# A streaming-encoder trunk in fp32: every other modulation unit of the first FFN's stage is loaded into the hf buffer

## Chip, cores and metric

One Trainium2 chip, one of its cores. The time is the device time of one execution in microseconds (us), the median of several runs.

## The reference

x is 256 frames of 1024 channels, c one vector of 1024. Two layers; in each a half-step SwiGLU FFN, a token mixer (layer 0 a pooling mixer, layer 1 a gated short convolution) and a second half-step FFN. Each of these three sub-layers is preceded by an RMS norm whose output is modulated from c:

```
cond = silu(c)
for i in range(2):
    mod = (cond @ ada_w[i] + ada_b[i]).reshape(B, 3, 3, 1024)
    shift, scale, gate = mod[:, :, 0], mod[:, :, 1], mod[:, :, 2]
    h = rms_norm(x, g[i, 0]) * (1 + scale[:, 0]) + shift[:, 0]
    a, b = split(h @ ffn_w_in[i, 0]);  x = x + 0.5 * gate[:, 0] * ((silu(a) * b) @ ffn_w_out[i, 0])
    ...   # the mixer, then the second FFN, in the same way
return rms_norm(x, final_g)
```

ada_w is 2 x 1024 x 9216; the hidden width of an FFN is 2816. Everything is fp32.

## The kernel before, in words

x lies transposed in SBUF, channels on 128 partitions in 8 blocks of 256 frames. All weights come from HBM in units of 1 MB, 128 partitions by 2048 elements (`UNIT`), one DMA each, all issued by SyncE (SP) in the order in which the program is written. SP issues in order: a DMA that has to wait for its buffer holds up those behind it. There are two sorts of units.

A weight unit goes through three engines. It lands in a buffer of the ring `raw` (4 buffers, `raw_unit`, L195). ACT casts it to a rounded `hi` (L239), DVE forms `lo = raw - hi` (L246, in the first product in two halves, L618 and L623), and PE multiplies three times for each product (`mm3`: hi with the high part hh of the activations, lo with hh, hi with the low part hl). The raw buffer is free when lo is done.

A modulation unit (`ada_unit`, L285, and `ada_first`, L289) lands in a buffer of the same ring. DVE alone reads it: `dot` (L262) multiplies it in place with cond and sums, two dots of 1024 elements a unit. Then its buffer is free.

The first FFN's first product (`ffn_start`) runs over the 8 blocks of channels (kb). Each block needs its own modulation unit (`ada_first(kb)`), from which DVE forms t (L359) and ACT hh (L360), and its weights. Block 0 is done in plain fp32: ACT writes the modulated activations into the buffer `hf`, and PE multiplies hf with the raw weights (16 products, 32 records in the profile). `second()` of a block is the second half of its work: for block 0 it copies hf into hh and hl (L608, L609), for the others it forms the second half of lo (L623) and issues the second half of the matmuls. It is called inside the next block's pass, so on DVE L623 of block 1 stands behind the dots and t of block 2:

```
for kb in range(KB):
    if kb:
        ada_first(kb)
    ...
    low_part = modulated(0, 0, kb, rstd, hh)
    second()
    low_part()
    high(1, 2)
    ...
```

The rest of the first FFN takes one weight unit after the other (14 more of its input weights, 11 of its output weights). In `swiglu` and `out_product`, `slot` calls `ada_unit` for later sub-layers, 18 units spread over 22 places, and 6 more come at the end of the stage. Each unit's DMA is written at the point of the program where its buffer is handed out.

hf (128 x 8 x 257 elements, L158) is used at the start for squares, then for block 0. Afterwards nothing touches it until, in the output product, `pool_shift_by_token` (L738) has ACT write the pooling mixer's shift into it (L741), and the stage's last residual writes the scaled x there.

Of the kernel before, what the change touches and what calls it, by code (L numbers as in the profile page):

```python
# [20 lines left out]
UNIT = 2048  # L21
# [96 lines left out]
def trunk(ctx: ExitStack, tc: tile.TileContext, calls, consts: bass.AP, c_in: bass.AP,  # L118
          x_in: bass.AP, fg_in: bass.AP, wall: bass.AP, out: bass.AP):
    nc = tc.nc  # L120
# [8 lines left out]
    def bank(name):  # L129
        return ps.tile([P, 2, T], F32, tag="bank", name=name)  # L130
# [4 lines left out]
    def mm(dst, w, m, start, stop):  # L135
        PE.matmul(dst, w, m, start=start, stop=stop, skip_group_check=True)  # L136

    def mm3(dst, w, m, start, stop):

        mm(dst, w[0], m[0], start, False)  # L140
        mm(dst, w[1], m[0], False, False)
        mm(dst, w[0], m[1], False, stop)
# [15 lines left out]
    hf = one.tile([P, KB, T + 1], F32, name="hf")  # L158
# [33 lines left out]
    gh = one.tile([P, FC, T], F32R, name="gh")  # L192
    gl = one.tile([P, FC, T], F32R, name="gl")

    def raw_unit(*call, tag="raw"):  # L195
        u = len(calls)
        calls.append(call)
        t = wp.tile([P, UNIT], F32, tag=tag, name=f"raw{u}", bufs=NRAW if tag == "raw" else NSPLIT)
        nc.sync.dma_start(t, wall[u])
        return t  # L200
# [6 lines left out]
    def unit(i):  # L207
        while len(units) <= i:
            call, at = todo.pop(0)
            if isinstance(at, str):  # L210
                raw = raw_unit(*call, tag=at)
                units.append((call, raw, None, None))
                continue
            raw = raw_unit(*call)
            if not gap:

                gap.append(wp.tile([P, BEHIND], F32, tag="gap", name="gap", bufs=1))
                G.memset(gap[0], 0.0)
            if at is None:
                parts = [wp.tile([P, UNIT], F32R, tag=n, name=f"{n}{len(units)}") for n in ("hi", "lo")]  # L220
            else:
                parts = [g[:, at : at + KB].rearrange("p b t -> p (b t)") for g in (gh, gl)]
            units.append((call, raw, *parts))
        return units[i]

    def spans(parts):
        n = UNIT // parts
        return [slice(p * n, (p + 1) * n) for p in range(parts)]
# [6 lines left out]
    def high(n, parts=1):  # L235

        for _, raw, hi, _ in next_of("hi", n):
            for at in spans(parts) if hi else ():
                S.copy(hi[:, at], raw[:, at])  # L239

    def low(n, parts=1):

        high(n, parts)
        for _, raw, hi, lo in next_of("lo", n):
            for at in spans(parts) if hi else ():
                V.tensor_sub(lo[:, at], raw[:, at], hi[:, at].bitcast(F32))  # L246

    def take(kind, pattern, **sizes):
        call, raw, hi, lo = units[done["used"]]
        assert call[0] == kind and done["lo"] > done["used"], (call, kind, done)  # L250
        units[done["used"]] = None
        done["used"] += 1
        if hi is None:
            return raw.rearrange(pattern, **sizes)
        return hi.rearrange(pattern, **sizes), lo.rearrange(pattern, **sizes)
# [8 lines left out]
    def mod_dots(layer, sub, mod, w, lo):  # L264

        key, n = (layer, sub, mod), w.shape[1]
        if key not in mods:
            mods[key] = one.tile([P, KB], F32, name=f"mod{layer}{sub}{mod}")
        b = ada_col(layer, sub, mod) + lo
        for i in range(n):  # L270
            dot(mods[key][:, lo + i : lo + i + 1], w[:, i], cst[:, b + i : b + i + 1])
        mod_finish(key, lo, n)

    def mod_finish(key, lo, n):
# [7 lines left out]
        elif mod == GATE and layer == 0:  # L282
            V.tensor_mul(m, m, cst[:, C_PS + lo : C_PS + lo + n])

    def ada_unit(layer, sub, mod, q):  # L285
        raw = raw_unit("ada", layer, sub, mod, q).rearrange("p (b n) -> p b n", b=2)
        mod_dots(layer, sub, mod, raw, 2 * q)

    def ada_first(kb):  # L289
        raw = raw_unit("ada0", kb).rearrange("p (m n) -> p m n", m=2)  # L290
        mod_dots(0, 0, SCALE, raw[:, 0:1], kb)
        mod_dots(0, 0, SHIFT, raw[:, 1:2], kb)

# [13 lines left out]
    def ada_next(n):  # L307
        for _ in range(n):
            ada_unit(*ada_todo.pop(0))
# [44 lines left out]
    def modulated(layer, sub, k, rstd, to):  # L354


        scale, shift = (mods[layer, sub, m][:, k : k + 1] for m in (SCALE, SHIFT))
        t = wk.tile([P, T], F32, tag="t", name=f"t{layer}{sub}{k}", bufs=4)
        V.scalar_tensor_tensor(t, x[:, k], scale, rstd, ALU.mult, ALU.mult)  # L359
        S.activation(to[:, k, :T], t, AF.Identity, bias=shift)  # L360
        return lambda: V.scalar_tensor_tensor(
            hl[:, k], t, shift, hh[:, k, :T].bitcast(F32), ALU.add, ALU.subtract
        )
# [10 lines left out]
    def h_pair(k):  # L374
        return hh[:, k, :T], hl[:, k]
# [179 lines left out]
    def swiglu_pair(cs, banks, name):  # L555
        sa, g = ({c: wk.tile([P, T], F32, tag=n, name=f"{n}{name}{c}") for c in cs} for n in ("sa", "g"))
        for c in cs:
            S.activation(sa[c], banks[c][:, 0], AF.Silu)
        for c in cs:
            V.tensor_mul(g[c], sa[c], banks[c][:, 1])  # L560
        for c in cs:
            S.copy(gh[:, c], g[c])
        for c in cs:
            V.tensor_sub(gl[:, c], g[c], gh[:, c].bitcast(F32))
# [17 lines left out]
    def ffn_start(rstd, name):  # L582

        banks = [bank(f"{name}b{c}") for c in range(NFIRST)]
        half = NFIRST // 2

        def product(kb, w, cs):
            for c in cs:
                for s in range(2):
                    mm3(banks[c][:, s], (w[0][:, c, s], w[1][:, c, s]), h_pair(kb),  # L590
                        kb == 0 and s == 0, kb == KB - 1)

        second = lambda: None
# [3 lines that stand above are left out]
            call, raw, hi, lo = unit(kb)  # L597
            if hi is None:
                modulated(0, 0, kb, rstd, hf)
                second()  # L600
                low(1)
                w = take("ffn_first", "p (c s n) -> p c s n", c=NFIRST, s=2)
                for c in range(NFIRST):
                    for s in range(2):
                        mm(banks[c][:, s], w[:, c, s], hf[:, kb, :T], kb == 0 and s == 0, kb == KB - 1)

                def second(kb=kb):
                    S.copy(hh[:, kb, :T], hf[:, kb, :T])  # L608
                    V.tensor_sub(hl[:, kb], hf[:, kb, :T], hh[:, kb, :T].bitcast(F32))  # L609

                continue
            low_part = modulated(0, 0, kb, rstd, hh)
# [3 lines that stand above are left out]
            done["lo"] += 1  # L616
            at, bt = spans(2)
            V.tensor_sub(lo[:, at], raw[:, at], hi[:, at].bitcast(F32))  # L618
            w = take("ffn_first", "p (c s n) -> p c s n", c=NFIRST, s=2)
            product(kb, w, range(half))  # L620

            def second(kb=kb, w=w, raw=raw, hi=hi, lo=lo):
                V.tensor_sub(lo[:, bt], raw[:, bt], hi[:, bt].bitcast(F32))  # L623
                product(kb, w, range(half, NFIRST))

        second()
        low(1)
        high(2)
        pairs = [lambda c=c: swiglu_pair((c, c + 1), banks, name) for c in range(0, NFIRST, 2)]
        pairs.pop(0)()  # L630
        low(2)
        high(3)
        ada_next(1)
        return NFIRST, pairs
# [57 lines left out]
    def ffn(layer, f, after, ahead, ready=lambda: None, between=lambda b: None, before=lambda u: None,  # L692
            rstd=None, groups=None, feed=None):
        sub, name = 2 * f, f"f{layer}{f}"
        if rstd:
            at, pairs = ffn_start(rstd, name)
        elif feed:
            at, pairs = ffn_fed(layer, f, sub, name, feed, 3, FILL)
        else:
            at, pairs = ffn_early(layer, f, sub, name, groups)  # L700
# [27 lines left out]
    def pool_means():  # L728
        S.copy(mh[:, :, 0, :EDGE], cst[:, C_E:C_M].rearrange("p (g v) -> p g v", g=4))
# [5 lines left out]
        V.tensor_mul(acc[:, :, :n], acc[:, :, :n], at)  # L735

    def pool_shift_by_token():
        pool_means()  # L738
        shift = mods[0, 1, SHIFT]
        for k in range(KB):  # L740
            S.activation(hf[:, k, :P], ones, AF.Identity, bias=shift[:, k : k + 1], scale=0.0)  # L741
# [137 lines left out]
    for p in range(2):  # L879
        b = bank(f"c{p}").rearrange("p a t -> p (a t)")  # L880
# [6 lines left out]
    rstd = rstd_of("s")  # L887
    table(AF.Silu)
    ada_first(0)

    steady = [4] * (LAST - 2)
# [74 lines left out]
```

## Time and profile before

| | us |
|---|---|
| runs shown | 863.17, 872.11, 862.32; median 863.17 |
| profiled execution | 863.46 |
| its span, first to last instruction | 861.5 |
| PE busy | 841.8 (98%) |
| DVE busy | 714.6 (83%) |
| ACT busy | 418.3 (49%) |
| granted TensorE clock, mean | 0.998 |
| read from HBM | 233.49 MB, 272 GB/s over the span |

PE's share counts matmuls from start to a modelled end, one overlapping the next, so a stretch in which PE looks busy is best judged by the number of its instructions in it. SPq rows are the issue of a DMA by SP; when it landed is another column. A wait is idle time of an engine, put down to what came last before it went on.

### The profile page before, as it was taken

What the parts mean: (1) busy time and instruction counts of PE and PEld (TensorE: products, weight loads), DVE (VectorE), ACT (ScalarE), POOL (GpSimd) and SP (SyncE); (2) the same over time, 40 slices, a digit from 0 to 9 for tenths busy, and PEclk for the clock granted to TensorE, in tenths of its full rate; (3) what the DMA queues carried; (4) which work ended last, traced back from release to release, by engine and by line L of the source; (5) the groups of instructions that cost most, each with busy time, mean ns of one, the idle gap of its engine ahead of it and who ended that gap; (6) DMA issues with size and microseconds to landing.
All of it is one profiled execution on the core that took longest, in us unless ns stands there. A gap on an engine that the chain in (4) does not pass through costs nothing.

```text
span 861.5 us, 16344 instructions
## 1 busy us (share of the span) xinstructions
PE 841.8 (98%) x6940; PEld 822.8 (96%) x6940; DVE 714.6 (83%) x1018; ACT 418.3 (49%) x538; POOL 8.4 (1%) x25
## 2 busy tenths in 40 slices
PE   4999999999999999999999999999999999999997
PEld 2999999999899999999999999999999999999886
DVE  6989999877889987878888988879887789755784
ACT  5355455343655444446644444356444756444422
POOL 3000000000000000000000000000000000000000
PEclk9999999999999999999999999999999999999999
DMA  8898899989548998886389989983465449954601
GB/s 343 335 344 322 301 350 379 370 347 385 178 165 320 372 341 321 350 310 237 105 331 350 377 310 337 363 321 148 161 228 180 190 145 343 331 192 165 224 22 49
DMA packets 33338, 235.59 MB, mean 273 GB/s; under 512 B 3697, under 2 KB 3825, under 8 KB 4978
## 3 DMA queue, kind: packets, MB, share of 16 engines
q1 hardware_dynamic: 33266, 234.56, 73.6%
q8 instruction: 54, 0.88, 0.4%
q14 instruction: 18, 0.15, 0.0%
HBM read 233.49 MB, written 1.05 MB: 272 GB/s over the span
## 4 chain that ended last, share of the span: by engine, by line
PE 85%; DVE 7%; DMA 5%; ACT 1%; issue 1%; SPq 0%; ACTq 0%
PE accf L136 21%; PE f01b L136 13%; PE f10b L136 13%; PE f11b L136 11%; PE acco L136 7%; PE f00b L136 4%; DMA raw<-wall 4%; PE pcv L136 4%; DVE raw L262 3%; PE accc L136 3%; DVE lo L246 2%; PE pe L136 2%; PE pb L136 2%; PE f01a L136 1%; PE f11a L136 1%; PE accz L136 1%
## 5 line engine op out<-in xcount | busy, mean ns | idle before, releaser
L239 ACT CAST hi<-raw 128x2048 fp32r<-128x2048 f32 (+1 forms) x151 | 263.9, 1762 | 132.5 <-DMA raw<-wall 77.5
L246 DVE TENSOR_TENSOR lo<-raw,hi 128x2048 fp32r<-128x2048 f32 (+1 forms) x137 | 298.9, 2194 | 33.1 <-ACT hi L239 32.9
L262 DVE CUSTOM_DVE_ANT_0 raw<-raw,cond,cst 128x1024 f32<-128x1024 f32 x144 | 179.6, 1281 | 12.5 <-DMA raw<-wall 12.2
L136 PE MATMUL accf<-gh,hi 128*128 128x256 f32 x528 | 145.9, 276 | 0.0
L136 PE MATMUL accf<-gh,lo 128*128 128x256 f32 x528 | 145.9, 276 | 0.0
L136 PE MATMUL accf<-gl,hi 128*128 128x256 f32 x528 | 145.8, 276 | 0.0
L136 PEld LDWEIGHTS accf<-gh,lo 128*128 128x128 f32 x528 | 99.1, 188 | 0.2
L136 PEld LDWEIGHTS accf<-gh,hi 128*128 128x128 f32 x528 | 99.1, 188 | 0.0
L136 PEld LDWEIGHTS accf<-gl,hi 128*128 128x128 f32 x528 | 99.1, 188 | 0.0
L136 PE MATMUL f00b<-hh,lo 128*128 128x256 f32 x336 | 93.1, 277 | 1.2 <-DVE lo L246 0.8
L136 PE MATMUL f00b<-hh,hi 128*128 128x256 f32 x336 | 93.1, 277 | 0.4 <-DVE gf L560 0.4
L136 PE MATMUL f00b<-hl,hi 128*128 128x256 f32 x336 | 92.8, 276 | 0.0
L136 PE MATMUL f11b<-hh,lo 128*128 128x256 f32 (+1 forms) x320 | 88.5, 277 | 0.3 <-DVE lo L246 0.3
L136 PE MATMUL f11b<-hh,hi 128*128 128x256 f32 (+1 forms) x320 | 88.4, 276 | 0.0
L136 PE MATMUL f11b<-hl,hi 128*128 128x256 f32 x320 | 88.4, 276 | 0.0
L136 PE MATMUL f10b<-hh,lo 128*128 128x256 f32 x320 | 88.3, 276 | 0.0
L136 PE MATMUL f10b<-hh,hi 128*128 128x256 f32 x320 | 88.3, 276 | 0.0
L136 PE MATMUL f10b<-hl,hi 128*128 128x256 f32 x320 | 88.3, 276 | 0.0
L136 PE MATMUL f01b<-hl,hi 128*128 128x256 f32 x304 | 84.6, 278 | 0.0
L136 PE MATMUL f01b<-hh,hi 128*128 128x256 f32 x304 | 84.2, 277 | 0.0
L136 PE MATMUL f01b<-hh,lo 128*128 128x256 f32 x304 | 83.9, 276 | 0.0
L136 PEld LDWEIGHTS f00b<-hh,lo 128*128 128x128 f32 x336 | 63.1, 188 | 1.8 <-DVE lo L246 1.0
(234 smaller groups left out, 1856.5 us busy)
## 6 DMA issues: line engine op xcount, KB each, us to landing
raw<-wall SPq DMA_DIRECT2D x221, 1024.0 KB, 6.0
x<-xt SPq DMA_DIRECT2D x4, 256.0 KB, 4.1
out<-x SPq DMA_DIRECT2D x4, 256.0 KB, 2.1
rows<-fg SPq DMA_DIRECT2D x1, 512.0 KB, 8.3
cst<-consts SPq DMA_DIRECT2D x1, 176.0 KB, 4.8
cond<-cvec SPq DMA_DIRECT2D x1, 4.0 KB
```

Of the source, the lines that this page charges most:

```text
L136: PE.matmul(dst, w, m, start=start, stop=stop, skip_group_check=True)
L239: S.copy(hi[:, at], raw[:, at])
L246: V.tensor_sub(lo[:, at], raw[:, at], hi[:, at].bitcast(F32))
L262: V.tensor_tensor_reduce(w, w, cond, 1.0, init, ALU.mult, ALU.add, out)
```

## The change

`raw_unit` gets an argument `home`: a buffer that it loads into in place of one of the ring. While a flag is on, every other call of `ada_unit` and `ada_first` passes the first 2048 elements of hf as home, the first call with the flag on included. The flag goes on in block 0's `second()`, behind the two instructions that read hf there, and off where `pool_shift_by_token` begins.

```diff
-    def raw_unit(*call, tag="raw"):
+    def raw_unit(*call, tag="raw", home=None):
         u = len(calls)
         calls.append(call)
+        if home is not None:
+            nc.sync.dma_start(home, wall[u])
+            return home
         t = wp.tile([P, UNIT], F32, tag=tag, name=f"raw{u}", bufs=NRAW if tag == "raw" else NSPLIT)
         nc.sync.dma_start(t, wall[u])
         return t
...
+    spare = {"on": False, "turn": 0}
+
+    def home():
+        if not spare["on"]:
+            return None
+        spare["turn"] += 1
+        return hf.rearrange("p k t -> p (k t)")[:, :UNIT] if spare["turn"] % 2 else None
+
     def ada_unit(layer, sub, mod, q):
-        raw = raw_unit("ada", layer, sub, mod, q).rearrange("p (b n) -> p b n", b=2)
+        raw = raw_unit("ada", layer, sub, mod, q, home=home()).rearrange("p (b n) -> p b n", b=2)
         mod_dots(layer, sub, mod, raw, 2 * q)
 
     def ada_first(kb):
-        raw = raw_unit("ada0", kb).rearrange("p (m n) -> p m n", m=2)
+        raw = raw_unit("ada0", kb, home=home()).rearrange("p (m n) -> p m n", m=2)
...
                 def second(kb=kb):
                     S.copy(hh[:, kb, :T], hf[:, kb, :T])
                     V.tensor_sub(hl[:, kb], hf[:, kb, :T], hh[:, kb, :T].bitcast(F32))
+                    spare["on"] = True
...
     def pool_shift_by_token():
+        spare["on"] = False
         pool_means()
```

The order of the weight transfers on SP stays; what they write and wait for changes. Before, from the first weight transfer on (raw0, raw2, raw4 and raw6 are the modulation units of blocks 0, 1, 2 and 3; raw1, raw3, raw5 and raw7 the weights of these blocks; in brackets the engines and earlier DMAs that a transfer waits for):

```order
L199 DMA raw0_148<-wall 128x2048
L199 DMA raw1_163<-wall 128x2048
L199 DMA raw2_184<-wall 128x2048 [waits DMAHW0_49]
L199 DMA raw3_189<-wall 128x2048 [waits DMAHW1_49]
L199 DMA raw4_228<-wall 128x2048 [waits DMAHW2_49]
L199 DMA raw5_233<-wall 128x2048 [waits DMAHW6_49,DMAHW3_49,DVE_49]
L199 DMA raw6_293<-wall 128x2048 [waits DMAHW4_49,DMAHW0_49,DVE_49]
L199 DMA raw7_298<-wall 128x2048 [waits DMAHW5_49,DMAHW2_49,DVE_49]
L199 DMA raw8_358<-wall 128x2048 [waits DMAHW1_49,DVE_49]
```

Of the changed kernel, the same place on SP:

```order
L202 DMA raw0_148<-wall 128x2048
L202 DMA raw1_163<-wall 128x2048
L202 DMA raw2_184<-wall 128x2048 [waits DMAHW0_49]
L202 DMA raw3_189<-wall 128x2048 [waits DMAHW1_49]
L199 DMA hf_82<-wall 128x2048 [waits DMAHW2_49,DVE_49,PE_49]
L202 DMA raw5_232<-wall 128x2048 [waits DMAHW3_49]
L202 DMA raw6_292<-wall 128x2048 [waits DMAHW6_49,DMAHW4_49]
L202 DMA raw7_297<-wall 128x2048 [waits DMAHW5_49,DMAHW0_49]
L199 DMA hf_82<-wall 128x2048 [waits DMAHW2_49,DVE_49]
```

The modulation unit of block 2, fifth in the row, waits for DVE and PE, and the three transfers behind it wait for no engine any more.

DVE of the changed kernel, from the end of block 1's first half on (mod001 and mod000 are the scale and shift of this sub-layer, t002 belongs to block 2, lo1 and lo2 are the low parts of the weights of blocks 1 and 2):

```order
L632 TENSOR_TENSOR lo1_194<-raw3_189,hi1_193 128x1024
L265 ISA hf_82,mod001_150<-hf_82,cond_73,cst_80 128x1024
L265 ISA mod001_150 128x1
L282 SCALAR_TENSOR_TENSOR mod001_150<-mod001_150,cst_80 128x1
L265 ISA hf_82,mod000_153<-hf_82,cond_73,cst_80 128x1024
L265 ISA mod000_153 128x1
L372 SCALAR_TENSOR_TENSOR t002_236<-x_75,mod001_150,rstds_142 128x256
L637 TENSOR_TENSOR lo1_194<-raw3_189,hi1_193 128x1024
L374 SCALAR_TENSOR_TENSOR hl_116<-t002_236,mod000_153,hh_115 128x256
L632 TENSOR_TENSOR lo2_235<-raw5_232,hi2_234 128x1024
```

Nothing moved on DVE; the two dots of block 2 read hf in place of raw4, and the second half of lo1 (L623 before, L637 now) stands behind them as it did.

## Rows read from the trace of the kernel before

**Rows 1.** The page, busy time of the engines: us, share of the span, instructions.
```profile
span 861.5 us, 16344 instructions
PE 841.8 (98%) x6940; PEld 822.8 (96%) x6940; DVE 714.6 (83%) x1018; ACT 418.3 (49%) x538; POOL 8.4 (1%) x25
```

**Rows 2.** The waits of PE in the whole span: engine and line, what it waited for, us in total, times, the longest.
```profile
PE f00b L136 <- ACT hf L360: 5.8, 1, 5.8
...
PE f00b L136 <- DVE lo L246: 0.8, 1, 0.8
PE f00b L136 <- DVE gf L560: 0.4, 1, 0.4
PE f00b L136 <- DVE lo L623: 0.4, 1, 0.4
PE f11b L136 <- DVE lo L246: 0.3, 1, 0.3
```

**Rows 3.** PE in two stretches: from:to, us, busy us (instructions), granted clock, DMA share, GB/s.
```profile
26.00:105.00 79.00, 77.35 (x675) 1.00 0.90 331
105.00:400.00 295.00, 295.00 (x2460) 1.00 0.87 324
```

**Rows 4.** The chain of work that ended last, in order of time: start, us, what.
```profile
104.69 38.27 PE f00b L136 x335
```

**Rows 5.** Waits for transfers of weights: engine and line, what it waited for, us in total, times, the longest.
```profile
ACT hi L239 <- DMA raw<-wall: 77.5, 34, 6.5
...
DVE raw L262 <- DMA raw<-wall: 12.2, 14, 1.8
```

**Rows 6.** Timeline of SP, single issues of weight transfers: start, us, engine, line, operation.
```profile
5.80 0.46 SPq L199 DMA_DIRECT2D raw<-wall  x1
...
15.50 0.33 SPq L199 DMA_DIRECT2D raw<-wall  x1
...
18.50 0.33 SPq L199 DMA_DIRECT2D raw<-wall  x1
...
24.54 0.33 SPq L199 DMA_DIRECT2D raw<-wall  x1
...
192.20 0.33 SPq L199 DMA_DIRECT2D raw<-wall  x1
192.62 1.65 SPq L199 DMA_DIRECT2D raw<-wall  x1
```

**Rows 7.** DMA issues in the windows of the issues at 5.80, 24.54, 192.20 and 192.62 us, in this order: size, us from issue to landing.
```profile
raw<-wall SPq DMA_DIRECT2D x1, 1024.0 KB, 14.6
...
raw<-wall SPq DMA_DIRECT2D x1, 1024.0 KB, 5.0
...
raw<-wall SPq DMA_DIRECT2D x1, 1024.0 KB, 5.2
...
raw<-wall SPq DMA_DIRECT2D x1, 1024.0 KB, 8.3
```

**Rows 8.** Timeline of DVE, blocks 1 to 3 and the low part of block 7: start, us, engine, line, operation, out<-in.
```profile
19.74 0.43 DVE L609 TENSOR_TENSOR hl<-hf,hh 128x256 fp32r<-128x256 f32 x1 [0.87 <-ACT hh L608]
...
21.83 1.28 DVE L262 CUSTOM_DVE_ANT_0 raw<-raw,cond,cst 128x1024 f32<-128x1024 f32 x1
...
24.43 0.48 DVE L359 SCALAR_TENSOR_TENSOR t<-x,mod,rstds 128x256 f32<-128x256 f32 x1
24.83 1.22 DVE L623 TENSOR_TENSOR lo<-raw,hi 128x1024 fp32r<-128x1024 f32 x1
25.97 0.47 DVE L361 SCALAR_TENSOR_TENSOR hl<-t,mod,hh 128x256 fp32r<-128x256 f32 x1
26.42 1.23 DVE L618 TENSOR_TENSOR lo<-raw,hi 128x1024 fp32r<-128x1024 f32 x1
27.57 1.28 DVE L262 CUSTOM_DVE_ANT_0 raw<-raw,cond,cst 128x1024 f32<-128x1024 f32 x1
...
33.33 1.28 DVE L262 CUSTOM_DVE_ANT_0 raw<-raw,cond,cst 128x1024 f32<-128x1024 f32 x1
...
56.97 1.23 DVE L618 TENSOR_TENSOR lo<-raw,hi 128x1024 fp32r<-128x1024 f32 x1
```

**Rows 9.** The instructions on the raw buffers up to 40 us, PE's matmuls of block 0 among them: count, ns min/median/max, first and last start in us.
```profile
L136 PE MATMUL f00b<-hf,raw x32: 379/379/794, 16.5 to 25.6; 128*128 128x256 f32 x32
```

**Rows 10.** PE in the stretch of block 1's first half, matmuls of f00b alone, columns as in rows 3.
```profile
25.60:28.30 2.70, 2.70 (x24) 1.00 0.87 322
```

**Rows 11.** PE around block 0, columns as in rows 3.
```profile
10.70:16.40 5.70, 0.00 (x0) 1.00 1.01 425
16.40:21.00 4.60, 4.54 (x11) 1.00 1.01 427
21.00:25.60 4.60, 4.60 (x23) 1.00 0.78 315
```

**Rows 12.** PE at the end of the span, columns as in rows 3.
```profile
855.00:856.00 1.00, 0.23 (x2) 1.00 0.45 176
...
857.00:858.00 1.00, 0.00 (x0) 0.74 0.00 0
858.00:859.00 1.00, 0.00 (x0) 0.50 0.14 55
```

**Rows 13.** Timeline of DVE, the first dots of two modulation units that land in hf in the changed kernel.
```profile
140.26 1.28 DVE L262 CUSTOM_DVE_ANT_0 raw<-raw,cond,cst 128x1024 f32<-128x1024 f32 x1
...
148.62 1.29 DVE L262 CUSTOM_DVE_ANT_0 raw<-raw,cond,cst 128x1024 f32<-128x1024 f32 x1
```

**Rows 14.** Timeline, DVE's step behind the last dots that the changed kernel makes in hf, and ACT's writes of the shift into hf.
```profile
176.36 0.16 DVE L283 TENSOR_TENSOR mod<-mod,cst 128x2 f32<-128x2 f32 x1
...
180.01 2.46 ACT L741 ACTIVATE hf<-ones,mod 128x128 f32<-128x128 f32 x8
```

## The prediction

> **What bounds the kernel now.** I read the page's busy shares first: TensorE (PE) is busy 98% of an 861.5 us span [rows 1]. A busy PE can still be a waiting one, so next came the list of waits, filtered to PE [rows 2]. The reader should see how short it is. Apart from the start (5.8 us until the first block's activations are there), the whole kernel holds four waits of PE, 0.8, 0.4, 0.4 and 0.3 us. Then I counted PE's instructions by stretch [rows 3]: 675 in the 79 us from 26 to 105 us, and from 105 to 400 us no idle time at all. In the chain that ended last, read in order of time, nothing but PE stands from 104.69 us on for hundreds of microseconds; its first piece gives PE's pace, 38.27 us for 335 matmuls, 0.114 us each [rows 4]. At that pace 79 us hold 692 matmuls, so 17 are missing, 1.9 us; the three waits in that stretch sum to 1.6 us, the same thing seen from the other side.
>
> So a better supply of weights in the first FFN can give back 1.6 us at most. A delay of PE in this stage, on the other hand, is passed on whole to the end, because there is no PE idle time behind it to absorb it. DVE and ACT do wait for transfers (12.2 and 77.5 us in all, [rows 5]), but those waits cost time only where PE waits behind them.
>
> **What the change moves.** The number of transfers, their size and all arithmetic stay as they are: 12 of the modulation units (blocks 2, 4 and 6 of the first product, and 9 later ones) land in hf and not in a raw buffer. Their dots have the same shape and I cost them at nothing (the rows of the dot below differ by 0.1 us at most, either way). The order list shows what does change. SP issues in order, and its fifth weight transfer, the modulation unit of block 2, now waits for PE and DVE, where before it waited for neither.
>
> *What it waits for.* Before, this transfer was issued at 5.80 us [rows 6] and landed 14.6 us later [rows 7], at 20.4 us, so DVE could begin its dot at 21.83 us with no wait [rows 8]. Now hf must first be free. Its last readers are DVE's subtraction at 19.74 us [rows 8], done at 20.2, and PE's 32 block-0 records, which run from 16.5 to 25.6 us plus 0.38 us [rows 9]. The later end decides: issue at 26.0 us, 20.2 us later than before. Behind it on SP stand the weights of block 2, the modulation unit of block 3 and the weights of block 3; before, these were issued at 15.5, 18.5 and 24.54 us [rows 6].
>
> *When it lands.* A transfer issued into a queue with little in it took 5.0 us (issue 24.54) and 5.2 us (issue 192.20); one issued 0.4 us behind that took 8.3 us [rows 6, 7], so they come through in order. At 26.0 us the queue is empty, since what went out ahead of this transfer had landed by 20.4 us. I take 5.0 us: hf has landed at 31.0 us, and the weights of block 2, the second of the burst, 8.3 us after 26.4, at 34.7 us. If it takes 8.3, add 3.3 us.
>
> *Who waits behind it.* DVE is in order too. Behind the two dots of block 2 stand t (L359) and then the second half of block 1's low part (L623), which PE needs for the second half of block 1. In the rows the dots start at 21.83, t at 24.43, L623 at 24.83, and the next step at 25.97 [rows 8]: 2.60, 0.40 and 1.14 us. From 31.0 us this gives 33.6, 34.0 and 35.1 us.
>
> *What PE does.* It starts block 1 at 25.6 us, and the 24 matmuls of its first half last until 28.3 us [rows 10]. Before, it went straight on. Now it stands until 35.1 us: a stall of 6.8 us. **Term 1: +6.8 us.**
>
> *The clock.* Twice the trace shows PE idle. From 10.7 to 16.4 us it did nothing; in the next 4.6 us it got through 11 records, in the 4.6 us after that through 23 of the same kind [rows 11]. The clock column says 1.00 in both, but the pace halves; I believe the pace. After the last matmul (in 855 to 856 us) the column itself shows 0.74 in 857 to 858 and 0.50, which is 1.2 GHz, from 858 us [rows 12]. An idle stretch of 6.8 us is longer than the one before 16.4 us, so I expect the same price after it: 12 records fewer in 4.6 us, or 2.4 us. **Term 2: +2.4 us**, bounds 0 (no fall) and 2.4. The Trainium skill (TensorE: Matmul & The Clock Gate, "Why this matters for your kernels") warns of drops to half clock after idle gaps between bursts of matmuls, the rule that speaks against this change; by it the sum holds term 2, without it the term is 0. The end of this trace agrees.
>
> *What comes back.* Block 2's low part starts 2.0 us after t does (24.43 to 26.42, with ACT's cast of weights between, which have just landed), so at 33.6 + 2.0 = 35.6 instead of 26.42 us: DVE is 9.2 us late. Per block DVE needs 5.76 us (27.57 to 33.33, [rows 8]), PE 48 x 0.114 = 5.5. Five more blocks put the low part of block 7 at 35.6 + 5 x 5.76 = 64.4 us, where before it was at 56.97 [rows 8]: 7.4 us late, since the small waits of DVE for transfers vanish on the way. PE is 9.2 us late when its stall ends at half clock, so it has become the later of the two and its three waits of 0.4, 0.4 and 0.8 us [rows 2] are swallowed. **Term 3: -1.6 us**, bounds 0 and -1.6.
>
> The sum is 6.8 + 2.4 - 1.6 = 7.6 us. Without the fall of the clock DVE decides: 7.4 us late at block 7, less the waits of 0.4 and 0.8 us behind it, 6.2 us. I take 7.5. The profiled execution took 863.46 us (its span and 2.0 us around it); 863.46 + 7.5 = 871.0 us. The median of before is 0.3 us lower than the profiled time, which I leave in the range.
>
> *Later parts that I cost at nothing.* The other 11 transfers into hf wait for the dots of the one before. Where two of them stand closest, the dots start at 140.26 and 148.62 us [rows 13]; the first end 2.6 us after their start, at 142.8, which leaves 5.8 us for the next transfer, against 5.0 to 5.2 us that it takes in a near-empty queue. The raw ring has the more room meanwhile. At the end of the stage ACT writes the shift into hf from 180.01 us; the last dots in hf end with DVE's step at 176.36 us [rows 14], 3.5 us earlier. If that cover went, the first of ACT's casts behind would be late by the difference.
>
> **The rivals.**
> *The hold ends early (not slower).* The list names the engine that a transfer waits for, not the instruction. If only DVE's subtraction holds it, the transfer goes at 20.2 and lands at 25.2 us; dots, t and L623 then end at 29.3 us, PE stalls 1.0 us with no fall of the clock, and 1.6 us come back: 863.46 - 0.6 = 862.9. The decisive point is the issue, 20.2 or 26.0 us. Against it: PE is named in the wait, and PE reads hf only in block 0. The Trainium skill (Perfetto Trace Analysis, "Optimization Strategy") reads repeated gaps as too few buffers, the rule in favour of the change; with no hold at all it would bring at most the 1.6 us of term 3, since PE hardly waits.
> *A dearer stall.* The four transfers that go out together share the engines, hf lands after 8.3 us rather than 5.0, and nothing comes back: 6.8 + 3.3 + 2.4 = 12.5, 876.0 us. For it: 8.3 was the second of a burst; against it: hf is the first.
> *Every hold costs (slower by over 2%).* If transfers into hf take 8.3 us in a full queue, they miss the 5.8 us by 2.5. Half of the 11 doing so on PE's path adds 13.8 us: 863.46 + 7.5 + 13.8 = 884.8. It decides where landing exceeds 5.8 us and PE has no lead. Against it: before, the fourth transfer back released the next, about the same event.
>
> **How the numbers follow.** Forecast 0.70, dearer stall 0.14, every hold 0.07, early end 0.09. Range 866.5 to 877.0: from 3 us above the profiled time before (terms 1 and 2 half as large, term 3 whole) to just beyond the dearer stall; it leaves out the early end and the third rival. A measurement of this kernel can tell about 2%, here 17 us, from no change: the forecast and the first two rivals lie within it, only the last is slower, and none is faster, as 1.6 us is all there is to win. Faster 0.01, same 0.92, slower 0.07.
>
> **What would show it.** The profile after should have a PE wait of about 7 us near 28 to 35 us, with L623 as its releaser and DVE's dot waiting some 6 us for a transfer; a first issue into hf near 26 us with three more right behind it; fewer matmuls in the 5 us after the stall than 44; PE's small waits up to 105 us gone; and from then on every stage shifted by one constant. The prediction is wrong if the first hf transfer goes out before 22 us, if PE is late by a further amount at 200 us than at 70 us, or if the time falls below 866 us.

## The result

The changed kernel takes 869.32 us (median of 21 runs, 868.26 to 870.08) against 864.15 us (median of the 21 runs of before beside it); the ratio of the runs is 1.0045, 95% interval 1.0024 to 1.0066. So it is slower, by 3.9 us by that ratio, by 5.2 us by these medians, and by 6.2 us from one profiled span to the other (861.5 to 867.7). The three differ because the runs of before scatter upwards, from 861.3 to 873.1 us, and those of the changed kernel hardly do. The forecast was 871.0 us, a loss of 7.5 us, which is under 2%.

The waits of PE in the profile after, columns as in [rows 2]:

```profile
PE f00b L136 <- DVE lo L637: 6.5, 1, 6.5
PE f00b L136 <- ACT hf L373: 5.8, 1, 5.8
...
PE f11b L136 <- DVE lo L249: 0.3, 1, 0.3
```

One new wait of 6.5 us has come, and the three of 0.8, 0.4 and 0.4 us are gone. The chain that ended last, in order of time (start, us, what), tells the new wait as a story; before, this chain ran mostly over DVE and transfers until PE alone took over in [rows 4]. f00b are the sums of the FFN's first product, accf those of its output product:

```profile
25.71 4.88 DMA hf<-wall
30.76 1.28 DVE hf L265
32.24 1.20 DVE hf L265
33.84 1.15 DVE lo L637
35.04 114.37 PE f00b L136 x983
149.40 48.96 PE accf L136 x432
```

The transfer goes out when block 0 is through, lands 4.9 us later, DVE makes its two dots, t and then block 1's low half, and only then PE goes on. From 35.04 us on it is PE alone. Before, the first accf row of the same view stands at 142.97 us:

```profile
142.97 49.20 PE accf L136 x432
```

So PE is 6.4 us late at the end of the FFN's first product, and 6.2 us late at the end of the kernel. DVE around the stall, timeline (start, us, operation, idle time before it), answering to [rows 8]:

```profile
30.76 1.28 DVE L265 CUSTOM_DVE_ANT_0 hf<-hf,cond,cst 128x1024 f32<-128x1024 f32 x1 [8.52 <-DMA hf<-wall]
...
33.76 1.22 DVE L637 TENSOR_TENSOR lo<-raw,hi 128x1024 fp32r<-128x1024 f32 x1
34.90 0.48 DVE L374 SCALAR_TENSOR_TENSOR hl<-t,mod,hh 128x256 fp32r<-128x256 f32 x1
35.36 1.23 DVE L632 TENSOR_TENSOR lo<-raw,hi 128x1024 fp32r<-128x1024 f32 x1
```

And PE in stretches (columns as in [rows 3], to be held against [rows 10, 11]):

```profile
28.30:31.00 2.70, 0.26 (x3) 0.92 0.99 416
31.00:34.00 3.00, 0.00 (x0) 0.50 1.01 426
36.00:40.60 4.60, 4.60 (x24) 0.50 1.02 427
40.60:45.20 4.60, 4.60 (x41) 0.98 0.99 408
105.00:400.00 295.00, 295.00 (x2462) 1.00 0.84 319
```

The clock falls to 0.50 (1.2 GHz) during the stall and stays there until about 40.8 us: 24 matmuls in 4.6 us against 41 in the next 4.6. PE looks fully busy in both.

### The profile page after: what moved, and what is told of

It reads as the page before. It is cut to its first block, busy times and chain, and to the rows that moved or that the text cites. A ratio compares the mean times of both kernels' runs of the same rounds, so it can differ in the third digit from the quotient of the medians.

```text
span 867.7 us, 16342 instructions
## 1 busy us (share of the span) xinstructions
PE 842.8 (97%) x6940; PEld 824.7 (95%) x6940; DVE 714.2 (82%) x1018; ACT 417.9 (48%) x538; POOL 7.4 (1%) x25
## 4 chain that ended last, share of the span: by engine, by line
PE 94%; DVE 3%; DMA 1%; ACT 1%; issue 0%; SPq 0%; DVEq 0%; ACTq 0%
PE accf L136 21%; PE f00b L136 14%; PE f01b L136 13%; PE f10b L136 13%; PE f11b L136 11%; PE acco L136 7%; PE pcv L136 4%; PE accc L136 3%; PE pe L136 2%; PE pb L136 2%; PE f01a L136 1%; PE f11a L136 1%; PE accz L136 1%; DVE lo L249 1%; PE f10a L136 1%; DMA hf<-wall 1%
## 5 line engine op out<-in xcount | busy, mean ns | idle before, releaser
L265 DVE CUSTOM_DVE_ANT_0 raw<-raw,cond,cst 128x1024 f32<-128x1024 f32 x120 | 149.5, 1280 | 7.4 <-DMA raw<-wall 7.3
```

The lines of the kernel that those rows point to most:

```text
L265: V.tensor_tensor_reduce(w, w, cond, 1.0, init, ALU.mult, ALU.add, out)
```

## The experiments

Four questions were left: whether the hold on the first transfer is the whole loss, what gives PE's small waits back, what the half clock costs on the path, and whether DVE's order matters.

**Only block 2's unit in hf** (e1_only_block2), so the hold without the later use:

```diff
-        return hf...[:, :UNIT] if spare["turn"] % 2 else None
+        return hf...[:, :UNIT] if spare["turn"] == 1 else None
```

> Only the modulation unit of block 2 goes to hf; all later units keep to the raw ring, as before the change. Theory (one stall in block 1, half clock behind it, and a delayed PE swallows its own small waits of 2.5 us whatever the buffers are): span 867 to 868.5 us, as with the whole change. Rival (the 11 later transfers into hf are what gives the 2.5 us back): 870 us. Rival (later holds cost, too): under 866 us.

Measured: span 870.5 us, ratio 1.0112 (1.0067 to 1.0158), runs 871.0 to 877.2 us. My theory fell; the first rival gave 870. Its waits of PE:

```profile
PE f00b L136 <- DVE lo L637: 7.5, 3, 6.6
...
PE f00b L136 <- DVE gf L573: 0.9, 1, 0.9
PE f00b L136 <- DVE lo L249: 0.3, 1, 0.3
```

The stall is there (6.6 us), and beside it the small waits, rather larger than before: 0.9 from two more on L637, 0.9 on gf (the gated activations) and 0.3, against 1.6 in all. A late PE does not swallow them. That DVE and the transfers are late with it is the likely reason, not a shown one; what is shown is that the 11 later transfers into hf, the only difference from the changed kernel, take them away.

**The later units in hf, block 2's in its raw buffer** (e2_from_block4):

```diff
-        return hf...[:, :UNIT] if spare["turn"] % 2 else None
+        return hf...[:, :UNIT] if spare["turn"] % 2 and spare["turn"] > 1 else None
```

> The modulation unit of block 2 stays in the raw ring; hf takes those of blocks 4 and 6 and the 9 later ones. Theory (the hold of the first transfer is the whole loss): no stall near 28 us, PE's waits up to 105 us (2.5 us by gaps between matmuls) mostly gone, span 859 to 861 us against 861.5, and a narrower spread of runs than before's. Rival (every transfer into hf costs): span over 863 us.

Measured: 860.08 us, ratio 0.9952 (0.9929 to 0.9975), span 858.3 us, a little under the 859 to 861 expected; 12 runs from 859.4 to 861.3. No stall; in the chain PE stands alone from its first record of block 0:

```profile
16.64 123.38 PE f00b L136 x1040
140.03 48.96 PE accf L136 x432
```

The accf row is 2.9 us earlier than before, 0.2 of it because block 0 ended earlier in this execution. This beats both kernels, and by more than the 1.6 us that I had called the most there is to win. The first transfer into hf still goes out only when block 0 is through, but it now stands four transfers further back, behind one that goes out at 24.72 us, so little is held:

```profile
24.72 0.33 SPq L202 DMA_DIRECT2D raw<-wall  x1
25.85 0.33 SPq L199 DMA_DIRECT2D hf<-wall  x1
```

The two halves of the change alone, and both, by span: neither 861.5, hold alone 870.5 (+9.0), later use alone 858.3 (-3.2), both 867.7 (+6.2). The parts add up to +5.8, near the whole, but these are single executions, and the parts are not the same in each: with the hold alone only 12 matmuls behind the stall ran at half clock, in the changed kernel 26.

```profile
35.28:37.90 2.62, 2.62 (x12) 0.50 1.04 363
```

**hf free from the start** (e3_hf_free): block 0's activations lie in a buffer of the tag `g`, unused there, and PE, ACT and DVE read them from it.

```diff
-                modulated(0, 0, kb, rstd, hf)
+                h0 = wk.tile([P, 1, T], F32, tag="g", name="h0")
+                modulated(0, 0, kb, rstd, h0)
...
-                        mm(banks[c][:, s], w[:, c, s], hf[:, kb, :T], kb == 0 and s == 0, kb == KB - 1)
+                        mm(banks[c][:, s], w[:, c, s], h0[:, kb], kb == 0 and s == 0, kb == KB - 1)
...
```

> As the changed kernel, but block 0's activations lie in a small tile of their own, so that hf is free once the squares at the start have been read (about 9.5 us), and the first transfer into hf need not wait for PE. Theory (PE's reading of hf is what holds SP): first issue into hf near 10 us, landing near 20 us, no stall, span 859 to 860.5 us. Rival (landing in hf or reading it is slower in itself): span over 864 us.

Measured: 859.89 us, ratio 0.9959 (0.9942 to 0.9975), span 857.9 us (859 to 860.5 expected). The first transfer into hf goes out at 9.30 us, in the timeline of SP, and lands 10.9 us later:

```profile
9.30 0.33 SPq L199 DMA_DIRECT2D hf<-wall  x1
```

With the same transfer into the same buffer and the readers of block 0 moved away, the loss is gone: the hold is its cause, not hf as a target. The edit moves DVE's reading away, too; that PE's was the one that held is read from the changed kernel, where DVE's subtraction from hf began at 20.06 us and the transfer went out at 25.71, at the end of block 0 on PE. Of the 3.6 us of span won, some 0.8 came from block 0 itself, which ended that much earlier in this execution.

**DVE's order** (e4_low_first): block 1's second half written ahead of block 2's dots.

```diff
+            if kb == 2:
+                second()
+                second = lambda: None
             if kb:
                 ada_first(kb)
```

> The changed kernel with the second half of block 1 (its low part on DVE and its matmuls) written ahead of the dots of block 2, so that it no longer stands behind the held transfer on DVE. Theory (PE's stall in block 1 comes from DVE's order): PE goes on to the end of block 1 near 31 us, stalls there until block 2's low part, which is due at the same 36.5 us as before, because ACT's cast and the dots set it: a stall of 5.4 in place of 6.65 us, span 866.3 to 867 us. Rival (the order on DVE does not matter, only when hf lands): 867.7 us; if the order were the whole cause: under 863 us.

Measured: span 867.8 us, time 869.25 us, ratio 1.0057 (1.0038 to 1.0075); the same as the changed kernel's, and the rival's number, not the 866.3 to 867 of my theory. PE did go on to the end of block 1, and then stalled for block 2:

```profile
PE f00b L136 <- ACT hi L242: 4.2, 1, 4.2
...
PE f00b L136 <- DVE lo L635: 0.7, 1, 0.7
PE f00b L136 <- DVE gf L573: 0.5, 1, 0.5
```

4.2 + 0.7 us in place of 6.5 brought next to nothing at the end: 0.5 came back as a wait for gf, and block 2's dots began 0.36 us later in this run (31.12 us); from there to accf it was 0.3 us quicker than the changed kernel. The order in DVE's queue moves the place of the stall; the time follows the landing of hf.

**The clock** (e5_zeros). Zero-weight matmuls, which add nothing to the sums, fill the stall:

```diff
...
+                for i in range(56 if kb == 1 else 0):
+                    mm(banks[half][:, 0], zero, hh[:, 0, :T], False, False)
                 product(kb, w, range(half, NFIRST))
```

> The changed kernel with 56 more matmuls of zero weights (6.3 us at 0.113) on PE between the halves of block 1, which fill its stall and add nothing to the sums. Theory (2.7 us of the loss are PE at half clock behind the stall): granted clock 1.00 throughout, no matmuls at 0.21 us behind 35 us, span 1.5 to 2.5 us under the changed kernel's, 865.2 to 866.2 us, where DVE becomes the limit. Rival (the clock costs nothing, DVE decides anyway): 867.5 us or more.

Measured: span 868.3 us, time 869.26 us, ratio 1.0058 (1.0033 to 1.0082). The clock stayed up:

```profile
28.00:35.00 7.00, 7.00 (x61) 1.00 0.94 378
35.00:40.00 5.00, 5.00 (x44) 1.00 1.00 421
```

yet the time is the changed kernel's. In part that is this run's start: block 0 ended later, and the dots of block 2 began at 31.98 us, 1.2 us after the changed kernel's; from there to accf it took 118.02 us, against 118.64. The rest shows in the chain, where PE now waits for DVE at the second half of each of the next blocks (a row of 5.73 us for 48 matmuls, where 48 x 0.1135 are 5.45):

```profile
42.51 5.72 PE f00b L136 x48
48.24 5.73 PE f00b L136 x48
...
65.48 84.51 PE f00b L136 x743
150.00 48.96 PE accf L136 x432
```

To have block 0 end alike, a pair got 44 more zero matmuls (128 columns) ahead of block 0, one without (e8_warm) and one with the filled stall (e7_warm_zeros).

```diff
         half = NFIRST // 2
+        for i in range(44):
+            mm(banks[0][:, 0, :P], zero, zero, True, True)
...
```

> The changed kernel with 44 small matmuls of zeros on PE ahead of block 0 (their results are overwritten), so that the clock is up when block 0 begins. Theory (the hold ends with block 0, and block 0's pace is set by the clock): block 0 ends near 23.4 us instead of 25.7, the first transfer into hf is issued then, everything behind is 2.3 us earlier, the stall and the fall of the clock behind it stay: span 865.2 to 866 us. Rival (hold not set by block 0): 867.7 us.

> As e8_warm, and with the 56 matmuls of zeros in the stall as well, so that the pair differs in the fall of the clock alone, with block 0 ending at the same time in both. Theory (half clock costs PE 2.7 us, but DVE's low part of block 6 lets PE keep at most 1.35 us of it): 1.0 to 1.4 us under e8_warm. Rival one (all 2.7 us are on the path): 2.7 us under it. Rival two (none is): the same.

Measured: 872.29 and 871.22 us, ratios 1.0095 (1.0075 to 1.0114) and 1.0080 (1.0058 to 1.0102), spans 870.1 and 869.5. The zeros missed their aim: the 44 matmuls took 9.4 us, where at 0.113 us each they would have taken 5.0, and block 0 behind them still began at half pace, at 19.7 and 20.1 us instead of 16.8. Nor did it end alike: the first transfer into hf went out at 29.25 and 28.23 us. The whole moved later, not earlier, so the expectation for the first is refuted in sign, though its mechanism is not: block 0's end still set the hold. The second is 1.1 us under the first by the medians, the number of my theory, but in the profiled executions its block 0 also ended 1.0 us earlier, so only the time from there on can tell. The chains, without and then with the filled stall:

```profile
34.23 1.28 DVE hf L265
...
38.51 113.22 PE f00b L136 x983
151.74 48.96 PE accf L136 x432
```

```profile
33.61 1.29 DVE hf L265
...
66.60 84.53 PE f00b L136 x743
151.13 48.96 PE accf L136 x432
```

From the first dot in hf to accf: 117.51 and 117.52 us, the same, which is the second rival's case. In the first of the pair the clock fell, but for a shorter while than in the changed kernel: 18 matmuls in the 3.5 us behind the stall, 13 fewer than at full pace, 1.4 us.

```profile
38.50:42.00 3.50, 3.49 (x18) 0.56 1.02 431
```

Nothing of that 1.4 shows. In the changed kernel 26 matmuls ran at half pace, which cost PE 2.6 to 2.7 us, and from the dot to accf it took 149.40 - 30.76 = 118.64 us: 1.1 us more than the pair, 0.6 more than the first run with the filled stall. The difference between these two is largely a wait of DVE for a transfer, which neither the pair nor the changed kernel has:

```profile
38.23 1.28 DVE L265 CUSTOM_DVE_ANT_0 raw<-raw,cond,cst 128x1024 f32<-128x1024 f32 x1 [0.41 <-DMA raw<-wall]
```

So about 1 us of the 2.7 stands on the path, from one execution of each kernel; the rest PE would have spent waiting for DVE.

**No hold, with the matmuls of zeros ahead of block 0** (e9_free_warm; the edit for hf free and the 44 matmuls, together):

> As e3_hf_free (block 0 in its own tile, no hold), with the 44 matmuls of zeros ahead of block 0. Theory (without a stall DVE's 5.75 us a block is the next limit of the first product): block 0 ends 1.5 to 2.3 us earlier, PE then waits for DVE at the second halves of the blocks, span 857.2 to 857.9 us against 857.9. Rival (PE alone is the limit there): 855.6 to 856.4 us.

Measured: 863.38 us, ratio 0.9999 (0.9985 to 1.0012), span 861.0 us; outside both. Block 0's records (count, ns, first and last start), first with the zeros ahead and then in the kernel with hf free:

```profile
L136 PE MATMUL f00b<-h,raw x32: 379/379/735, 19.9 to 28.0; 128*128 128x256 f32 x32
```

```profile
L136 PE MATMUL f00b<-h,raw x32: 379/379/796, 16.3 to 24.7; 128*128 128x256 f32 x32
```

It ended 3.3 us later, and the span grew by 3.1. Without a hold, lateness of block 0 passes on almost whole, and PE's list has no wait behind block 0 in this product in either run, so PE is the limit there. What I had asked, whether DVE becomes the limit once block 0 ends earlier, stays open, since it ended later.

## Why the prediction was right, and where it was not

*The hold and the stall (term 1, +6.8).* Right in every step: issue at 25.71 us (forecast 26.0), landing 4.9 us later (5.0), dots at 30.76 (31.0), PE on again at 35.04 (35.1). In the changed kernel the gap was 6.76 us from one matmul's start to the next, 0.11 of them its ordinary pace: 6.65. What the forecast did not have: PE began block 1 some 0.3 us earlier than in the run of before. DVE's low part of block 7 began at 64.10 us, forecast 64.4.

*The clock (term 2, +2.4).* The fall came and cost PE 2.6 to 2.7 us, as the idle stretch ahead of block 0 had suggested; the Trainium skill's warning (TensorE: Matmul & The Clock Gate, "Why this matters for your kernels") agrees with the 0.50 of the row above. But only about 1 us of it stands on the path, as the filled stalls show. I had put the two limits beside each other (7.6 with the fall, 6.2 without) and so had nearly this size, 1.4.

*What comes back (term 3, -1.6).* Wrong in cause and size. I took the sum of PE's listed waits. A wait is listed only as far as it outlasts the modelled end of the matmul before it: the listed 0.81 us at 104.69 is 1.08 us from start to start, where 0.11 is the pace, so 0.97 us were lost:

```profile
103.61 0.28 PE L136 MATMUL f00b<-hh,hi 128*128 128x256 f32 x1
104.69 0.39 PE L136 MATMUL f00b<-hh,lo 128*128 128x256 f32 x1 [0.81 <-DVE lo L246]
```

Summed over all such places from 26 to 105 us, the waits were 2.6 us, not 1.6. My count of missing matmuls had pointed the same way, and I read its 1.9 us as the same as 1.6; at the pace of the accf row (48.96 us for 432) it gives 2.5. And the waits went because of hf as a fifth buffer beside the ring's four, not because PE was late: with the hold alone they stayed. From this follow two wrong sentences of the prediction, that a better supply can give back 1.6 us at most, and that PE hardly waits; the later use alone won 3.2 us of span, 2.7 of it between the start of block 1 and accf. The rule of the Trainium skill that I weighed and set aside (Perfetto Trace Analysis, "Optimization Strategy": the same gap again and again can mean too few buffers) agrees: with one buffer more these 2.6 us of gaps are gone.

*The sum.* 6.65 - 0.3 + 2.7 - 2.6 = 6.4 us at the accf row, forecast 7.6. The smaller loss is term 3's missing microsecond and the start, which is chance. This counts PE's own time and so holds the 2.7 whole; at full clock most of it would have come back as waits for DVE.

*The rivals.* No early end: the issue came when PE was through with block 0. No dearer stall: hf landed first of the burst. Later holds cost nothing: PE has no further wait in this stage. What stays open is why the runs of before, and those of the kernel with the hold alone, scatter by several us, while those of the kernels with the later transfers in hf lie within 2 us; that slack in the transfers evens them out fits all of these, but no profile of a long run was taken.

## What to carry to other kernels

A buffer that is idle later is not idle yet: before a transfer is sent into it, ask which engine reads it last and when, and count everything behind that transfer in the issuing queue as held until then. The same buffer taken one turn later, or emptied of its last reader, turned a loss of 6.2 us of span into a gain of 3.2 to 3.6, of which 2.5 to 2.7 are PE's small waits and the rest is mostly the earlier end of block 0 in these executions. The waits that PE showed here were too short, since its matmuls' ends are modelled; count matmuls or compare starts.

## What was not expected of the hardware

A stream of 44 matmuls of zeros, 128 columns each, on an otherwise idle PE took 9.4 us, 0.22 us each, and block 0 behind it began at half pace all the same (the rows are of e9_free_warm):

```profile
10.50:19.50 9.00, 9.00 (x44) 1.00 1.01 428
19.70:24.00 4.30, 4.30 (x15) 1.00 1.01 429
24.00:28.00 4.00, 4.00 (x20) 1.00 1.01 420
```

The clock column says 1.00 throughout; the pace of the records does not. From start to start, 4, 6 and 11 records of block 0 ran at half pace in the three runs with these zeros, 8 to 13 in the seven without. In contrast, 56 matmuls of zero weights with real activations in a stall, on a PE that was already up, kept the clock at 1.00. Whether the operands or the state before made the difference was not tried.
